# Order of the query tiles within an attention head: long and short tiles in turn instead of ascending

## The chip, the cores and the metric

One Trainium2 chip, one of its cores. The metric is the device time of one execution of the whole program, in microseconds (us); of several executions the median is given. Engines are named as the profile names them: PE is TensorE (PEld its weight loads), DVE VectorE, ACT ScalarE, POOL GpSimd, SP the queue that issues most DMAs. TensorE runs at one of two clock levels, 2.4 GHz and 1.2 GHz; the profile shows which was granted.

## The reference

Two decoder layers over 1024 tokens of width 1024, batch 1, in float32. Each layer projects the normed input once and splits the result among three token mixers: MLA attention (4 heads), GLA and RWKV-7; their outputs are joined, projected and added, and a gated convolutional FFN follows. The change is in the attention, which is causal, in query blocks of 128:

```python
for i in range(S // Q_BLOCK):
    end = (i + 1) * Q_BLOCK
    qb = q[:, i * Q_BLOCK:end]
    s = jnp.einsum('bqhd,bkhd->bhqk', qb, k[:, :end], preferred_element_type=jnp.float32)
    mask = (i * Q_BLOCK + local)[:, None] >= jnp.arange(end)[None, :]
    p = jax.nn.softmax(jnp.where(mask, s, -jnp.inf), axis=-1)
    outs.append(jnp.einsum('bhqk,bkhd->bqhd', p.astype(v.dtype), v[:, :end]))
```

Query block i meets i+1 key blocks, so block 7 is eight times the work of block 0. The blocks do not depend on each other.

## The kernel before

The program is one function, run once for each of the two layers: input projections, then a stage in which attention and the RWKV-7 recurrence run together, then the output projection (line 1424), then the FFN. The change touches the middle stage alone.

In that stage the outer loop goes over the 4 heads (h) and the inner one over the 8 query tiles (i). For a tile, `scores` writes q times k into a two-bank PSUM tile `psb` with matmuls of at most 512 columns (line 97; five for each run of columns, three of them `kn,qn` and two of them `khh,QP` and `kll,QP`). There are two such `psb` tiles. DVE adds the causal mask (L1119), takes the row maximum (L1121) and scales it (L1122); ACT takes the exponential into `p` (L1124). `trans` transposes `p` on PE, 128 columns at a time (L1135), and `pv` multiplies by v (L1146). The three run one tile apart: after the scores of a tile come the transposes of the tile before and the `pv` of the one before that (`flush`). A tile with i+1 key blocks asks for i+1 transposes and i+1 `pv` products. A `pv` product is a float32 matmul, which the trace records twice.

The weights of the next head are loaded and split by `dense_w` (L990, L992, L994) after the fourth tile of a head, and multiplied at its last tile (`dense_k`, `dense_q`).

The RWKV-7 recurrence is a generator, `rwkv_chunks`, over 8 pairs of chunks. It is resumed step by step: `spend` adds an estimate of PE time after each piece of attention, in proportion to i+1, and resumes the generator once for each 0.9 of it. Its steps are many small matmuls (L807, L821/L822, L832, L838, L852, L862, L879, L896, L900, L926) with a DVE or ACT step between them: L821 and L822 transpose in two groups of four, each into its own PSUM tile `psr`, DVE copies a group out (L825), and L832 follows; L807 is masked by DVE into `SC` (L811, two of them), which L879 reads. There are two `psr` tiles. When the heads are done, `drain` runs out what is left.

In head 3 a second generator, `early_wout`, prepares the output projection, which begins with tokens 0 to 127.

The order in which a loop records instructions is not the order in which an engine runs them: the framework schedules all engines by a simulated timeline and then fixes each engine's order. So PE's order in this stage is a mixture of attention, recurrence and projections, and a changed loop order moves all of it.

Of the kernel before, what the change touches and what calls it, by code (L numbers as in the profile page):

```python
# [21 lines left out]
NT = T // 128  # L22
# [39 lines left out]
def trunk(ctx: ExitStack, tc: tile.TileContext, A, out, offs):  # L62
# [241 lines left out]
    for l in range(DEPTH):  # L304
# [692 lines left out]
        def pg(tag, name, dt=F32, bufs=1):  # L997
            return ap.tile([128, T], dt, tag=tag, name=name, bufs=bufs)
# [83 lines left out]
        def dense_w(h):  # L1082
            return (w_small(2, 128, [(0, WKV[:, 256 * h:256 * h + 128])]),
                    w_small(3, 128, [(0, WQ[:, 192 * h:192 * h + 128])]))

        def dense_k(h, w):
            ps = bigps()
            mtile(ps, 128, 2, w, ckv)
            ps = halves(ps)
            kn = [pg(f"kn{j}", f"kn{j}", F32R) for j in range(2)]  # L1090
            for n in range(2):
                N = HALF[n]
                dve.tensor_tensor(ps[n], ps[n], Rk[:, N], ALU.mult)
                act.activation(kn[0][:, N], ps[n], AF.Copy)
                dve.tensor_tensor(kn[1][:, N], ps[n], kn[0][:, N].bitcast(F32), ALU.subtract)
            return kn

        def dense_q(h, w):
            ps = bigps()
            mtile(ps, 128, 3, w, cq)  # L1100
            ps = halves(ps)
            qn = [pg(f"qn{j}", f"qn{j}", F32R) for j in range(2)]
            for n in range(2):
                N = HALF[n]
                act.activation(qn[0][:, N], ps[n], AF.Copy)
                dve.tensor_tensor(qn[1][:, N], ps[n], qn[0][:, N].bitcast(F32), ALU.subtract)
            return qn

        def scores(h, i):
            kn, qn, qp = heads[h]  # L1110
            tk = slice(i * 128, (i + 1) * 128)
            nk = (i + 1) * 128
            s = bigps()
            for n0 in range(0, nk, 512):
                ks = slice(n0, min(max(nk, n0 + 256), n0 + 512))
                mm3(s[:, ks], (qn[0][:, tk], qn[1][:, tk]), (kn[0][:, ks], kn[1][:, ks]), True, False)
                mmr(s[:, ks], qp[:, tk], khh[:, ks], False, False)
                mmr(s[:, ks], qp[:, tk], kll[:, ks], False, True)
            dve.tensor_tensor(s[:, tk], s[:, tk], C("mdiag"), ALU.add)  # L1119
            sm = ap.tile([128, 4], F32, tag="sm", name="sm", bufs=4)  # L1120
            dve.tensor_reduce(sm[:, 0:1], s[:, 0:nk], AX.X, ALU.max, negate=True)  # L1121
            dve.tensor_scalar(sm[:, 1:2], sm[:, 0:1], rq[:, i:i + 1], None, ALU.mult)  # L1122
            p = pg("P", "p", bufs=2)
            act.activation(p[:, 0:nk], s[:, 0:nk], AF.Exp, scale=rq[:, i:i + 1], bias=sm[:, 1:2], accum_out=sm[:, 2:3])  # L1124
            dve.reciprocal(sm[:, 3:4], sm[:, 2:3])
            spend(0.27 * (i + 1))
            return p, sm
# [69 lines left out]
        def early_wout():  # L1197
            for k in range(3):
                wout_w(k)
                yield  # L1200
                yield
            prep_load(0)
            for k in range(3, 5):
                wout_w(k)
                yield
                yield
# [5 lines left out]
        def flush(n):  # L1212
            nonlocal t1, t2
            if n and t1 is not None:
                nt = (*t1[:2], trans(t1[1], t1[2]), t1[3])
            else:
                nt = None
            if t2 is not None:
                pv(*t2)
            t1, t2 = None, nt  # L1220

        for h in range(4):
            for i in range(NT):
                if h == 3 and i == 0:
                    bg.append(early_wout())
                r = scores(h, i)
                if h < 3 and i == 3:
                    wts = dense_w(h + 1)
                if i == NT - 1 and h < 3:
                    kn = dense_k(h + 1, wts[0])  # L1230
                    flush(1)
                    t1 = (h, i, *r)
                    qn = dense_q(h + 1, wts[1])
                    if h == 0:
                        heads[1] = (kn, qn, QP[1])
                        Q2 = [None, None]
                        Q2[0] = pg("QP0", "QPr", F32R)
                        nc.sync.dma_start(out=Q2[0].bitcast(F32), in_=qdr[0])
                    elif h == 1:
                        heads[2] = (kn, qn, Q2[0])  # L1240
                        Q2[1] = pg("QP1", "QPr", F32R)
                        nc.sync.dma_start(out=Q2[1].bitcast(F32), in_=qdr[1])
                    else:
                        heads[3] = (kn, qn, Q2[1])
                else:
                    flush(1)
                    t1 = (h, i, *r)
# [521 lines left out]
```

## Time and profile before

| what | us |
|---|---|
| median of 3 runs | 2701.03 |
| lowest and highest of them | 2699.57, 2706.45 |
| the profiled execution | 2708.75 |
| span of its profile | 2707.0 |
| PE busy in the span | 2620.6 (97%) |
| DVE busy | 1693.5 (63%) |
| ACT busy | 1145.0 (42%) |
| POOL busy | 1040.7 (38%) |

The profile is of one execution, and times in its rows are us from the start of its span. A busy PE is not a PE at its peak: matmuls are pipelined, their ends are modelled, and a matmul at 1.2 GHz is busy twice as long. The stage of the change runs from about 371 to 595 us in layer 0 and from about 1712 to 1940 us in layer 1.

### The profile page before, as it was taken

What the parts mean: (1) busy time and instruction counts of PE and PEld (TensorE: products, weight loads), DVE (VectorE), ACT (ScalarE), POOL (GpSimd) and SP (SyncE); (2) the same over time, 40 slices, a digit from 0 to 9 for tenths busy, and PEclk for the clock granted to TensorE, in tenths of its full rate; (3) what the DMA queues carried; (4) which work ended last, traced back from release to release, by engine and by line L of the source; (5) the groups of instructions that cost most, each with busy time, mean ns of one, the idle gap of its engine ahead of it and who ended that gap; (6) DMA issues with size and microseconds to landing.
All of it is one profiled execution on the core that took longest, in us unless ns stands there. A gap on an engine that the chain in (4) does not pass through costs nothing.

```text
span 2707.0 us, 35550 instructions
## 1 busy us (share of the span) xinstructions
PE 2620.6 (97%) x13586; PEld 2129.8 (79%) x13586; DVE 1693.5 (63%) x2404; ACT 1145.0 (42%) x1880; POOL 1040.7 (38%) x907
## 2 busy tenths in 40 slices
PE   8999999999999999999999999999999999999997
PEld 7668788888778888777776787888887788887786
DVE  3446565555976666777733665556469766668785
ACT  4221244454444544533352223444544454545433
POOL 3446432232554444221234553222325554542311
PEclk9999989999999999999999999799999999999999
DMA  4102121133232222684411122211332222216951
GB/s 130 32 24 68 56 70 41 33 126 125 78 100 73 94 72 70 210 202 119 122 30 32 32 71 70 54 34 42 129 130 66 94 84 80 94 55 220 211 129 63
DMA packets 246267, 240.90 MB, mean 89 GB/s; under 512 B 40312, under 2 KB 188240, under 8 KB 246096
## 3 DMA queue, kind: packets, MB, share of 16 engines
q1 hardware_dynamic: 210752, 203.31, 23.5%
q0 software_dynamic: 14336, 27.27, 5.8%
q10 hardware_dynamic: 21008, 8.04, 1.2%
q8 instruction: 107, 1.75, 0.3%
q14 instruction: 64, 0.52, 0.1%
HBM read 178.80 MB, written 53.48 MB: 86 GB/s over the span
## 4 chain that ended last, share of the span: by engine, by line
PE 76%; DVE 10%; DMA 4%; issue 4%; ACT 3%; POOL 3%; SPq 0%; POOLq 0%; DVEq 0%; ACTq 0%
PE psb L97 24%; PE psr L97 19%; PE psa L97 17%; PE psa L1146 2%; DMA R<-in_ffn_w_down 2%; PE psa L1135 1%; DMA R<-fdr 1%; PE psr L896 1%; PE psr L862 1%; PE psr L807 1%; DVE Tb L701 1%; DVE Ttmp L699 1%; DVE RG L1282 1%; PE psa L503 1%; PE psr L900 1%
## 5 line engine op out<-in xcount | busy, mean ns | idle before, releaser
L97 PE MATMUL psb<-hh,wh 128*128 128x512 f32 (+2 forms) x704 | 266.3, 380 | 5.3 <-ACT acc L748 3.9
L97 PE MATMUL psb<-hl,wh 128*128 128x512 f32 (+2 forms) x704 | 269.2, 383 | 1.6 <-DVE hl L208 1.6
L97 PE MATMUL psb<-hh,wl 128*128 128x512 f32 (+2 forms) x704 | 268.6, 382 | 1.8 <-POOL wl L258 1.8
L97 PE MATMUL psr<-B,RG 128*128 128x512 f32 x1032 | 253.9, 391 | 0.2
L97 PE MATMUL psa<-T,RG 128*128 128x512 f32 x1008 | 247.3, 391 | 1.0 <-ACT RG L1281 1.0
L97 PEld LDWEIGHTS psr<-B,RG 128*128 128x128 f32 x1032 | 193.4, 188 | 43.2 <-DVE RG L1282 1.0
L1282 POOL TENSOR_TENSOR RG<-S_m,RG 128x512 fp32r<-128x512 f32 x86 | 121.4, 1411 | 274.2 <-ACT RG L1281 239.5
L97 PEld LDWEIGHTS psa<-T,RG 128*128 128x128 f32 x1008 | 189.7, 188 | 42.8 <-ACT RG L1281 1.8
L1281 ACT ACTIVATE RG<-S_m 128x512 fp32r<-128x512 f32 x176 | 111.0, 630 | 227.0 <-PE psa L97 119.1
L97 PEld LDWEIGHTS psb<-hh,wh 128*128 128x128 f32 (+1 forms) x704 | 132.0, 188 | 35.0 <-issue 4.9
L97 PEld LDWEIGHTS psb<-hh,wl 128*128 128x128 f32 (+1 forms) x704 | 132.1, 188 | 34.4 <-issue 10.5
L97 PEld LDWEIGHTS psb<-hl,wh 128*128 128x128 f32 (+1 forms) x704 | 132.3, 188 | 29.6 <-issue 5.4
L97 PE MATMUL psr<-T,RG 128*128 128x512 f32 x528 | 137.4, 402 | 11.0 <-ACT T L1281 9.2
L97 PEld LDWEIGHTS psr<-T,RG 128*128 128x128 f32 x528 | 101.9, 194 | 35.7 <-ACT T L1281 10.1
L258 POOL TENSOR_TENSOR wl<-ws,wh 128x1024 fp32r<-128x1024 f32 (+1 forms) x40 | 91.2, 2281 | 95.8 <-ACT wh L256 61.3
L1479 DVE SCALAR_TENSOR_TENSOR psb<-uv,convc,psb 128x1023 f32<-128x1023 f32 x72 | 92.6, 1287 | 55.2 <-ACT psb L1477 54.2
L1281 ACT ACTIVATE de<-R 128x1024 fp32r<-128x1024 f32 x67 | 69.1, 1052 | 123.0 <-DMA R<-fdr 40.7
L1282 DVE TENSOR_TENSOR de<-R,de 128x1024 fp32r<-128x1024 f32 x67 | 86.2, 1303 | 43.9 <-ACT de L1281 43.9
L1589 POOL DMA_DIRECT2D R<-fdr x48 | 44.6, 982 | 176.8 <-issue 45.8
L97 PE MATMUL psb<-de 128*128 128x512 f32 x384 | 107.6, 399 | 5.0 <-DVE acc_kb L1660 5.0
L1479 DVE SCALAR_TENSOR_TENSOR psb<-ug,convc,psb 128x1023 f32<-128x1023 f32 x72 | 92.4, 1283 | 24.9 <-ACT psb L1477 23.9
L254 POOL TENSOR_TENSOR ws<-ws,pcol 128x1024 f32<-128x1024 f32 x36 | 74.3, 2068 | 82.3 <-DMA ws<-in_w_in 78.0
(549 smaller groups left out, 6626.0 us busy)
## 6 DMA issues: line engine op xcount, KB each, us to landing
wu_m<-in_ffn_w_up SPq DMA_DIRECT2D x88, 512.0 KB
fdr<-acc SPq DMA_DIRECT2D x44, 512.0 KB
R<-fdr SPq DMA_DIRECT2D x88, 256.0 KB
R<-in_ffn_w_down SPq DMA_DIRECT2D x88, 256.0 KB
ws<-in_w_in SPq DMA_DIRECT2D x38, 512.0 KB
R<-fdr POOLq DMA_DIRECT2D x48, 256.0 KB, 6.5
y_m<-ydr SPq DMA_DIRECT2D x16, 512.0 KB
xmid<-x SPq DMA_DIRECT2D x16, 512.0 KB
```

Of the source, the lines that this page charges most:

```text
L97: pe.matmul(o, lhsT=l, rhs=r, start=first, stop=last, skip_group_check=on)
L254: eng.tensor_tensor(ws, ws, g.rearrange("p (k o) -> p k o", o=1).to_broadcast([128, K, M]), ALU.mult)
L258: eng.tensor_tensor(wl, ws, wh.bitcast(F32), ALU.subtract)
L503: pe.matmul(pu[:, 0:256], lhsT=keT[r, i, :], rhs=vT[i // 4][r, i % 4, :], start=True, stop=True)
L699: dve.tensor_tensor(t3, Tb[:, 0:k, k:k + 1].to_broadcast([128, k, w]), Ub[:, k:k + 1, k + 1:32].to_broadcast([128, k, w]), ALU.mult)
L701: dve.tensor_tensor(Tb[:, 0:k, k + 1:32], Tb[:, 0:k, k + 1:32], t3, ALU.add)
L807: pe.matmul(pss[h2][:, o:o + 128], lhsT=kb[hf][p // 4][rows, 2 * (p % 4) + cc].rearrange("p a s -> p (a s)"), rhs=var[hf][p // 4][rows, 2 ...
L1146: pe.matmul(po[:, 0:128], lhsT=pT[:, j * 128:(j + 1) * 128], rhs=v[:, j, h * 128:(h + 1) * 128], start=(j == 0), stop=(j == i))
L1281: act.activation(d[0], s, AF.Copy)
L1282: eng.tensor_tensor(d[1], s, d[0].bitcast(F32), ALU.subtract)
L1479: dve.scalar_tensor_tensor(a[:, d:T], u[:, 0:T - d], conv[:, 2 - d, jj:jj + 1], a[:, d:T], ALU.mult, ALU.add)
L1589: pool.dma_start(out=o, in_=x, accum_op=ALU.add)
```

## The change

Within heads 0 to 2 the tiles go 7, 0, 6, 1, 5, 2, 4, 3, and within head 3 they go 0, 7, 1, 6, 2, 5, 3, 4. What was tied to the first, the fourth or the last tile of a head is tied to the first, fourth or last place in the new order. No arithmetic changes.

```diff
+
+        MIX = (7, 0, 6, 1, 5, 2, 4, 3)
         for h in range(4):
-            for i in range(NT):
-                if h == 3 and i == 0:
+            for n, i in enumerate(MIX if h < 3 else (0, 7, 1, 6, 2, 5, 3, 4)):
+                if h == 3 and n == 0:
                     bg.append(early_wout())
                 r = scores(h, i)
-                if h < 3 and i == 3:
+                if h < 3 and n == 3:
                     wts = dense_w(h + 1)
-                if i == NT - 1 and h < 3:
+                if n == NT - 1 and h < 3:
                     kn = dense_k(h + 1, wts[0])
                     flush(1)
                     t1 = (h, i, *r)
```

Every engine runs the same instructions as before, in another order within this stage. Three places matter below. The first is PE at the start of head 0 in layer 0 (`rcb` and `SC` are the recurrence's buffers, `kn`, `qn`, `khh`, `kll` and `QP` hold keys and queries). Before:

```order
L852 MATMUL psr<-rcb 32x32 x8
L97 MATMUL psb<-kn_2649,qn_2788 128x256
L97 MATMUL psb<-kn_2650,qn_2788 128x256
L838 MATMUL psr<-rcb,SC 64x64 x8
L97 MATMUL psb<-kn_2649,qn_2789 128x256
L896 MATMUL psr<-rcb,SC 128x64 x4
L900 MATMUL psr<-St_2340,rcb 128x128 x2
L862 MATMUL psr<-rcb 64x128 x4
L97 MATMUL psb<-kn_2649,qn_2788 128x256
L97 MATMUL psb<-kn_2650,qn_2788 128x256
L97 MATMUL psb<-kn_2649,qn_2789 128x256
L862 MATMUL psr<-rcb 64x128 x4
```

After:

```order
L852 MATMUL psr<-rcb 32x32 x8
L838 MATMUL psr<-rcb,SC 64x64 x8
L896 MATMUL psr<-rcb,SC 128x64 x4
L900 MATMUL psr<-St_2340,rcb 128x128 x2
L862 MATMUL psr<-rcb 64x128 x4
L97 MATMUL psb<-kn_2649,qn_2788 128x512
L97 MATMUL psb<-kn_2650,qn_2788 128x512
L97 MATMUL psb<-kn_2649,qn_2789 128x512
L97 MATMUL psb<-kn_2649,qn_2788 128x256
L97 MATMUL psb<-kn_2650,qn_2788 128x256
L97 MATMUL psb<-kn_2649,qn_2789 128x256
L862 MATMUL psr<-rcb 64x128 x4
```

The six 256-column score matmuls of tiles 0 and 1 have become three of 512 (first half of tile 7) and three of 256 (tile 0), in one run. The second place follows a little later on PE, from the first matmuls with `QP` on. Before:

```order
L97 MATMUL psb<-khh,QP_2495 128x256
L97 MATMUL psb<-kll,QP_2495 128x256
...
L807 MATMUL psr<-t_va_524,t_kb_520 128x128
L1135 MATMUL psa<-cst,p 128x128
L97 MATMUL psb<-kn_2649,qn_2788 128x384
L97 MATMUL psb<-kn_2650,qn_2788 128x384
L97 MATMUL psb<-kn_2649,qn_2789 128x384
L97 MATMUL psb<-khh,QP_2495 128x384
L97 MATMUL psb<-kll,QP_2495 128x384
L879 MATMUL psr<-SC,rcb 64x128 x6
```

After, ahead of and behind the same eight L807 matmuls:

```order
L97 MATMUL psb<-khh,QP_2495 128x512
L97 MATMUL psb<-kll,QP_2495 128x512
L97 MATMUL psb<-kn_2649,qn_2788 128x512
L97 MATMUL psb<-kn_2650,qn_2788 128x512
L97 MATMUL psb<-kn_2649,qn_2789 128x512
L97 MATMUL psb<-khh,QP_2495 128x512
L97 MATMUL psb<-kll,QP_2495 128x512
L97 MATMUL psb<-khh,QP_2495 128x256
L97 MATMUL psb<-kll,QP_2495 128x256
...
L879 MATMUL psr<-SC,rcb 64x128 x8
L926 MATMUL psr<-g2s,t_sg 128x256
L1135 MATMUL psa<-cst,p 128x128 x8
```

Ahead of L807 stand 4096 score columns where there were 1024 (four matmuls of 256); behind it nothing stands between L807 and L879. DVE's order there, after the change:

```order
L1121 TENSOR_REDUCE sm<-psb 128x1
L1119 TENSOR_TENSOR psb<-psb,cst 128x128
L929 TENSOR_TENSOR rcb<-rcb,st 128x256
L811 TENSOR_TENSOR SC<-psr,cst 128x4x128
L1122 TENSOR_SCALAR sm<-sm,rq 128x1
L1121 TENSOR_REDUCE sm<-psb 128x1
L811 TENSOR_TENSOR SC<-psr,cst 128x4x128
```

Two steps of the softmax, L1122 and L1121, stand between the two L811. The third place is PE at the last chunk pair of the recurrence. Before (the same in both layers):

```order
L1135 MATMUL psa<-cst,p 128x128 x3
L1146 MATMUL psa<-v,pT 128x128 x2
L821 MATMUL psr<-cst,t_va_523 128x128
L822 MATMUL psr<-cst,hat 128x128
L821 MATMUL psr<-cst,t_va_525 128x128
...
L822 MATMUL psr<-cst,hat 128x128
L832 MATMUL psr<-rcb,SC 32x32 x8
L838 MATMUL psr<-rcb,SC 64x64 x8
```

After, in layer 1:

```order
L821 MATMUL psr<-cst,t_va_10747 128x128
L822 MATMUL psr<-cst,hat 128x128
L821 MATMUL psr<-cst,t_va_10749 128x128
L822 MATMUL psr<-cst,hat 128x128
L1146 MATMUL psa<-v,pT 128x128
L97 MATMUL psb<-kn_14740,qn_14784 128x256
L97 MATMUL psb<-kn_14741,qn_14784 128x256
L97 MATMUL psb<-kn_14740,qn_14785 128x256
L97 MATMUL psb<-khh,QPr 128x256
L97 MATMUL psb<-kll,QPr 128x256
L832 MATMUL psr<-rcb,SC 32x32 x8
```

Before, the eight L821/L822 run straight into L832; after, a `pv` product and a tile's scores stand between (in layer 0 thirteen projection matmuls and a transpose do).

## Rows read from the trace of the kernel before

**Rows 1.** The page's first part: busy us, share of the span, instructions.

```profile
PE 2620.6 (97%) x13586; PEld 2129.8 (79%) x13586; DVE 1693.5 (63%) x2404; ACT 1145.0 (42%) x1880; POOL 1040.7 (38%) x907
```

**Rows 2.** Busy time by stretch: stretch, length, engines in the order named, granted clock, DMA.

```profile
core 0: us, PE busy (x) PEld busy (x) DVE busy (x) ACT busy (x) POOL busy (x), PEclk, DMA share, GB/s
372.71:389.77 17.06, 16.93 (x75) 14.78 (x73) 12.54 (x25) 6.00 (x13) 4.04 (x5) 0.50 0.05 12
1714.14:1738.04 23.90, 23.77 (x100) 19.79 (x101) 15.40 (x37) 7.84 (x18) 7.24 (x9) 0.50 0.05 12
1898.46:1901.88 3.42, 3.42 (x14) 3.13 (x13) 0.00 (x0) 3.32 (x8) 1.33 (x3) 0.50 0.05 19
389.80:595.00 205.20, 203.55 (x1619) 177.44 (x1618) 118.76 (x309) 101.34 (x227) 54.57 (x79) 1.00 0.19 60
1738.00:1895.00 157.00, 156.52 (x1263) 136.49 (x1262) 91.30 (x242) 74.37 (x172) 34.81 (x51) 1.00 0.13 38
```

**Rows 3.** Whom PE waited for, layer 0's stage: total us, times, longest.

```profile
PE psr L832 <- DVE SC L825: 0.8, 1, 0.8
PE psa L1135 <- ACT p L1124: 0.5, 1, 0.5
```

**Rows 4.** PE in order of time, layer 0's start: start us, us, work [idle before].

```profile
371.85 1.28 PE L838 MATMUL psr<-rcb,SC 64*64 64x64 f32 x16
...
379.02 1.96 PE L862 MATMUL psr<-rcb 64*64 64x128 f32 x8
381.12 1.97 PE L896 MATMUL psr<-rcb,SC 128*128 128x64 f32 x8
...
383.70 0.56 PE L97 MATMUL psb<-khh,QP 128*128 128x256 f32 x1
...
384.83 3.09 PE L807 MATMUL psr<-t_va,t_kb 64*128 64x128 f32 x16
...
387.99 1.31 PE L97 MATMUL psb<-kn,qn 128*128 128x384 f32 x3
...
389.85 0.63 PEld L879 LDWEIGHTS psr<-SC,rcb 64*64 64x64 f32 x12 [0.42 <-DVE rcb L929]
```

**Rows 5.** PE in order of time, the same place in layer 1.

```profile
1724.49 0.56 PE L97 MATMUL psb<-khh,QP 128*128 128x256 f32 x1
...
1736.95 1.36 PE L97 MATMUL psb<-kn,qn 128*128 128x512 f32 x3
```

**Rows 6.** Groups by shape on DVE and ACT, layer 0's stage: busy us, mean ns | idle.

```profile
L1119 DVE TENSOR_TENSOR psb<-psb,cst 128x128 f32<-128x128 f32 x32 | 9.4, 298 | 13.8 <-PE psb L97 13.3
L811 DVE TENSOR_TENSOR SC<-psr,cst 128x512 f32<-128x512 f32 x12 | 8.3, 689 | 2.8 <-PE psr L807 2.6
L1122 DVE TENSOR_SCALAR sm<-sm,rq 128x1 f32<-128x1 f32 x32 | 6.5, 210 | 0.5
L1121 DVE TENSOR_REDUCE sm<-psb 128x1 f32<-128x1024 f32 x4 | 4.9, 1225 | 0.8 <-ACT o L1149 0.7
L1121 DVE TENSOR_REDUCE sm<-psb 128x1 f32<-128x128 f32 x4 | 1.2, 291 | 0.1
L1124 ACT ACTIVATE p<-psb,sm,rq 128x1024 f32<-128x1024 f32 x4 | 4.8, 1203 | 0.4 <-DVE sm L1122 0.3
```

**Rows 7.** PE in order of time at full clock, layer 0, head 0 to 1.

```profile
442.15 1.08 PE L862 MATMUL psr<-rcb 64*64 64x128 f32 x8
443.16 1.10 PE L896 MATMUL psr<-rcb,SC 128*128 128x64 f32 x8
...
447.22 1.16 PE L807 MATMUL psr<-t_va,t_kb 64*128 64x128 f32 x8
```

**Rows 8.** PE in order of time, last chunk pair of layer 1.

```profile
1895.47 0.27 PE L822 MATMUL psr<-cst,hat 128*128 128x128 f32 x1
1896.57 0.69 PE L832 MATMUL psr<-rcb,SC 32*32 32x32 f32 x16 [0.83 <-DVE SC L825]
```

**Rows 9.** POOL in order of time: the weight split for a coming head.

```profile
428.57 1.00 POOL L994 TENSOR_TENSOR wl<-ws,wh 128x384 fp32r<-128x384 f32 x1 [0.27 <-ACT wh L992]
```

## The prediction

> **What bounds the kernel now.** I read the busy shares first [rows 1]: PE is busy for 97% of the span. A share over the whole span says little about one stage, so I read busy time by stretch next. From 389.80 to 595 us of layer 0 PE is busy 203.55 of 205.20 us at full clock, and from 1738 to 1895 us of layer 1 156.52 of 157.00 us; DVE and ACT lie below 60% in both [rows 2]. The waits of PE confirm it: in layer 0's whole stage the view names 0.8 us behind L825 and 0.5 us behind the exponential [rows 3]. The reader should see that the stage is bound by PE, that the recurrence and the projections fill what the softmax leaves open, and that an order of tiles cannot make PE's list shorter: every tile asks for the same matmuls in either order.
>
> What an order can change is the rate at which PE works off its list. Here the stretches tell something the waits do not: from 372.71 to 389.77 us and from 1714.14 to 1738.04 us the granted clock was 0.50, that is 1.2 GHz, though PE was busy 16.93 of 17.06 and 23.77 of 23.90 us; a third such stretch of 3.42 us lies at 1898.46 [rows 2]. PE at half clock does half the work, so these three cost 8.5, 12.0 and 1.7 us. In time order they begin while PE runs the recurrence's narrow matmuls (L838 on 64 rows and 64 columns, L862) with short score matmuls between them [rows 4], the third behind a wait of 0.83 us [rows 8]; the clock is back after the 384-column scores that begin at 387.99 us in layer 0 [rows 4] and during a run of 512-column scores in layer 1 [rows 5]. The change is worth what it makes of these three places.
>
> **The start of head 0.** Between L838 and the first `QP` matmul the order now holds the same recurrence and 3 x 512 + 3 x 256 = 2304 score columns instead of 6 x 256 = 1536. 768 columns more at 1.2 GHz are 0.64 us, so the `QP` matmuls, which began at 383.70 and 1724.49 us [rows 4, 5], now begin near 384.3 and 1725.1. There follow 7 x 512 + 2 x 256 = 4096 score columns without a break, 3.4 us at 1.2 GHz, to 387.7 and 1728.5. Such a run is what stood at the clock's return before; I take it that the clock is back at its end. Low clock would then end 2.1 us sooner in layer 0 and 9.5 us in layer 1, 11.6 us in all, of which half, **5.8 us, is won**. If the run does not bring the clock back, nothing is won: the bounds are -5.8 and 0.
>
> The columns drawn ahead are missed behind L807. Before, the five 384-column matmuls stood between L807 and L879 and covered DVE's masking; L879 waited 0.42 us [rows 4]. Now L879 follows L807 directly, and on DVE stand L811, L1122, L1121 of tile 0, L811: 0.689 + 0.210 + 0.291 + 0.689 = 1.88 us [rows 6]. Behind L879 are queued L926 and tile 7's eight transposes, so all of PE waits. 1.88 - 0.42 = 1.46 us in each layer, **2.9 us lost**. A wait of this size is what preceded the third low stretch [rows 8], and narrow L879 follows it, so the clock may fall again: a stretch of 3.42 us costs 1.7. I take **1.7 us** for one of the two layers, with bounds of 0 and 3.4.
>
> **The end of the recurrence.** The wait of L832 for L825 (0.8 us in layer 0, 0.83 in layer 1 [rows 3, 8]) comes from eight L821/L822 that run straight into L832. The new order has other matmuls between them at this place in both layers: 1.6 us won. The low clock at 1898.46 follows this wait; if it goes too, 1.7 more. **-3.3 us**, bounds -3.3 and 0. The wait can move to another chunk pair, but nowhere in the new order do the eight run undivided into L832.
>
> **Tile 7's softmax.** Where a long tile was followed by a long one, it is now followed by a short one, and its chain has less cover: mask 0.298, maximum 1.225, scaling 0.210, exponential 1.203, together 2.94 us [rows 6]. I counted in the new order what PE has between tile 7's last wide score matmul and its first transpose. In head 1 of layer 0, the tightest kind: five 256-column scores of tile 0, two L862 of 8 records, an L896, an L900 and four L807. The rows of these shapes give 2 x 1.08 + 1.10 + 1.16 = 4.4 us without scores and L900 [rows 7]. So 1.5 us of slack remain. If another DVE job is in the way, a wait like the 0.5 us of [rows 3] returns; I take one, **+0.5 us**, with bounds of 0 and 4 (one in each of eight heads).
>
> **Edits costed at nothing.** The weights of the next head are recorded after 18 of 36 key blocks instead of 10. Their split ends with 1.00 us on POOL [rows 9], and half a head, some 25 us of a 205 us stage with four heads [rows 2], still covers it; uncovered it would be about 1 us for each of six heads. The attention's output DMAs are as many as before. Their last tile is now tile 4, where it was tile 7, but tiles 0 and 1, which the output projection takes first, are still among the first three, and tile 4 waits behind four tiles of 48 matmuls each, 10 us a tile at 2.4 GHz. The background steps are resumed as often in a head, only earlier in it.
>
> **Sum.** -5.8 + 2.9 + 1.7 - 3.3 + 0.5 = -4.0 us. On the profiled execution's 2708.75 us that is 2704.8; that execution lies 7.7 us above the median shown, 2701.03, so against the median I expect **2697**. The bounds add up to -6.2 (-5.8 + 2.9 - 3.3) and +10.3 (2.9 + 3.4 + 4). 0.3% is 8.1 us, about what a measurement of this kernel can tell from no change.
>
> **Rivals.** *The clock returns at the first run already (19%).* The six matmuls of 2304 columns ahead of the second L862 could suffice. They would end about 4.7 us before the `QP` matmuls, since the second L862 and an L896 take 4.7 us from 379.02 to 383.70 [rows 4], near 379.6 and 1720.4. Then 10.2 + 17.6 us of low clock go, half of it won: -13.9 + 2.9 - 3.3 + 0.5 = -13.8, 2687. For it: a run of this length stands nowhere in the low stretch before. Against it: narrow L862 and L896 follow at once.
>
> *Long tiles are no longer covered (8%, slower).* If the real softmax chain is slower than the fixed order allows, each long tile stops PE between its scores and its transposes. Without the recurrence, a tile of 5 x 256 columns covers 0.5 us of 2.94. Half of the remaining 2.4 us on the four long tiles of eight heads is 32 x 1.2 = 38 us, less 4.0: 2735. It decides from 0.4 us a tile on (8.1 + 4.0 over 32). Against it: the fillers counted above, and the 0.5 us of [rows 3].
>
> *A new low stretch (4%, slower).* If the wait at L879 brings down the clock for as long as before, 17 us in each layer, 17 us are lost and only the end is won: 2701 + 17 + 2.9 - 3.3 = 2718.
>
> *PE's busy time hides waits (4%, faster).* The weight loads are busy 177.44 us where the matmuls are busy 203.55, and 136.49 where they are 156.52 [rows 2]. If this difference, 26.1 + 20.0 = 46 us, were waits inside matmuls, a smoother order could win part of it; a third is 15 us, 2686.
>
> The Trainium skill says so of the measure: its page "Trainium Kernel Development and Optimization", section "Performance Expectations", calls matmul busy time a bad metric of how near a kernel is to its limit, because matmuls are pipelined, and points to the busy share of the weight loads. By that rule the sum would start from 46 us of room in place of none. The trace bears it out only in part: loads are below matmuls in every stretch, but the view of waits names some 1.3 us.
>
> *The forecast: no change that can be told (65%)*, 2693 to 2709. That the order stays what it was is excluded; it does move on every engine.
>
> **How the numbers follow.** Faster by over 0.3%: 19 + 4 = 23%. Slower: 8 + 4 = 12%. The same: 65%. The range reaches down to 2686, into the first rival, and up to 2711, the upper bound of the sum; outside lie the slower rivals and little of the faster ones.
>
> **What the profile after would show.** Right: low clock in layer 1's start ends near 1729, not 1738; L879 idles near 1.9 us behind L811; no wait of L832 for L825 at the last chunk pair; PE busy over 99% between. Wrong: waits of L1135 for the exponential that add up to several us; a low stretch behind L879; low clock as long as before.

## The result and the profile after

The changed kernel takes 2725.89 us (median of four runs, 2722.38 to 2731.97), the kernel before 2702.26 on the same chip (2699.57 to 2706.45): a ratio of 1.0079, 95% interval 1.0062 to 1.0096. It is slower, by more than the 0.3% that can be told here. Measured a second time, on another occasion, the ratio is 1.0064 (1.0048 to 1.0080), 15.0 us between the medians (f1 below). I had forecast 2697 and no change that can be told.

The profiled execution after has a span of 2720.6 us, the one before 2707.0: 13.6 us to explain. The first part of the page after answers [rows 1]:

```profile
PE 2619.9 (96%) x13586; PEld 2128.9 (78%) x13586; DVE 1690.9 (62%) x2404; ACT 1142.5 (42%) x1880; POOL 1045.7 (38%) x907
```

PE is busy as long as before (2620.6). What was not busy is 2707.0 - 2620.6 = 86.4 us before and 2720.6 - 2619.9 = 100.7 after, 14.3 us more, and the mean granted clock is 0.979 in both. So the loss is idle time of PE; the next question is where.

To compare the two I cut both programs at the same amounts of PE work: I added up, in PE's order, the usual distance from one matmul to the next at full clock (0.227 us for one of 512 columns, and so on), and looked up when PE reached a given sum. For each layer's attention that gives three stretches: the start (sums 250 to 310, and 1480 to 1550 in layer 1), the middle (to 440, 1640) and the end (to 520, 1720), which reaches into the output projection. Busy time by stretch, the kernel before, first layer 0, then layer 1 (stretch, length, then busy us of the engines, granted clock, DMA):

```profile
322.90:400.20 77.30, 74.34 (x486) 61.46 (x484) 44.27 (x82) 36.03 (x73) 31.49 (x36) 0.87 0.29 77
400.20:543.00 142.80, 142.32 (x1150) 123.88 (x1147) 80.57 (x212) 65.05 (x150) 29.48 (x44) 1.00 0.12 36
543.00:627.60 84.60, 83.11 (x544) 71.39 (x544) 45.33 (x92) 43.59 (x85) 27.10 (x41) 1.00 0.39 131
...
1690.70:1781.70 91.00, 88.87 (x640) 75.67 (x639) 53.08 (x123) 42.02 (x93) 25.45 (x31) 0.85 0.19 52
1781.70:1881.10 99.40, 98.92 (x784) 85.19 (x783) 56.37 (x149) 45.73 (x105) 21.29 (x32) 1.00 0.12 33
1881.10:1967.70 86.60, 85.11 (x571) 74.02 (x570) 48.35 (x101) 44.14 (x89) 25.62 (x37) 0.98 0.36 119
```

The same pieces of work after the change:

```profile
323.40:399.50 76.10, 69.29 (x493) 57.17 (x492) 43.32 (x76) 33.78 (x65) 31.49 (x36) 0.93 0.29 76
399.50:541.70 142.20, 142.14 (x1163) 123.98 (x1162) 80.49 (x220) 64.20 (x152) 34.92 (x52) 1.00 0.11 31
541.70:633.30 91.60, 85.78 (x525) 72.84 (x523) 47.18 (x90) 46.75 (x91) 21.64 (x33) 0.98 0.39 130
...
1698.20:1786.20 88.00, 83.99 (x630) 71.63 (x629) 52.12 (x118) 39.02 (x86) 26.58 (x31) 0.90 0.19 53
1786.20:1889.20 103.00, 101.64 (x805) 88.81 (x803) 57.61 (x157) 44.00 (x107) 24.54 (x37) 0.97 0.09 24
1889.20:1980.70 91.50, 86.07 (x560) 73.04 (x559) 49.51 (x99) 46.47 (x93) 22.91 (x34) 0.98 0.37 122
```

The reader should see three things. The starts became shorter, by 1.2 and 3.0 us. The middle is as it was in layer 0 (142.8 and 142.2) and 3.6 us longer in layer 1. The ends became longer by 7.0 and 4.9 us, and there PE idles 5.82 and 5.43 us where it idled 1.49 each time. The rest of the program is 2.9 us longer. The sum is 13.6.

What PE waits for in layer 0's stage (total us, times, longest), to be read against [rows 3] (the view before also lists shorter waits of 0.5, 0.3 and 0.3 us in that stage, which [rows 3] leaves out):

```profile
PE psr L879 <- DVE SC L811: 2.5, 2, 2.3
PE psb L97 <- ACT p L1124: 2.4, 2, 1.5
...
PE psr L97 <- ACT RG L1176: 1.2, 1, 1.2
PE psa L1146 <- ACT pT L1137: 0.9, 1, 0.9
PE psr L97 <- DVE RG L1177: 0.5, 1, 0.5
```

L879 lies at the start of the stage. The other four are new and lie at its end. PE in order of time at the end of layer 0's stage, after the change:

```profile
567.34 0.97 PE L97 MATMUL psb<-kn,qn 128*128 128x512 f32 x3 [0.90 <-ACT p L1124]
...
572.15 0.71 PE L1146 MATMUL psa<-v,pT 128*128 128x128 f32 x4 [0.86 <-ACT pT L1137]
...
574.68 1.65 PE L97 MATMUL psb<-kn,qn 128*128 128x512 f32 x3 [1.49 <-ACT p L1124]
...
591.44 2.17 PE L1146 MATMUL psa<-v,pT 128*128 128x128 f32 x18
593.36 0.95 PE L97 MATMUL psr<-wo_kb,yhl_m 128*128 128x512 f32 x3
595.52 0.73 PE L97 MATMUL psr<-RG,yhl_m 128*128 128x512 f32 x2 [1.21 <-ACT RG L1176]
```

Scores wait until an exponential has read one of the two score buffers `psb`; then the output projection waits for its weights in `RG`, the blocks that can be written only once the attention's buffers are free. ACT there, first before the change, then after:

```profile
586.63 0.37 ACT L1149 ACTIVATE o<-psa,sm 128x128 f32<-128x128 f32 x1 [1.42 <-PE psa L1146]
...
587.40 2.01 ACT L1176 ACTIVATE RG<-wos 128x1024 fp32r<-128x1024 f32 x2 [0.40 <-DMA x<-in_x]
```

```profile
593.64 0.37 ACT L1149 ACTIVATE o<-psa,sm 128x128 f32<-128x128 f32 x1 [0.75 <-PE psa L1146]
...
594.41 2.01 ACT L1176 ACTIVATE RG<-wos 128x1024 fp32r<-128x1024 f32 x2 [0.40 <-ACT o L1149]
```

In both, `RG` is copied right behind the last output `o` of the attention. What differs is what PE has left to do meanwhile. PE before the change:

```profile
583.08 3.51 PE L1146 MATMUL psa<-v,pT 128*128 128x128 f32 x30
586.34 2.33 PE L97 MATMUL psr<-wo_m,yhl_m 128*128 128x512 f32 x9
588.51 1.04 PE L204 MATMUL psb<-cst,y_m 128*128 128x128 f32 x8
...
590.76 2.97 PE L97 MATMUL psr<-RG,yhl_m 128*128 128x512 f32 x12
```

Before, 15 L97 and 8 L204, 4.2 us, stood between the attention's last product and the first matmul on `RG`; after, three L97, 0.95 us. The others had been drawn ahead to fill the last tiles, because something else was no longer there. Counted in PE's fixed order of layer 0, 38 rows of attention and projection follow the recurrence's last L926 before the change, up to the attention's last L1146, and 130 follow it after. The recurrence's last L926 stands after 472 us of PE work before and after 460 after the change: it runs ahead, and the last tiles lose their filler.

Layer 1 is not the same. There the last L926 stands only some 3 us of work earlier after the change, and 77 rows follow it up to the last L1146 (38 before). No scores wait for an exponential; PE waits for the recurrence's own state and for the projection's weights:

```profile
PE psr L900 <- DVE St L904: 1.8, 1, 1.8
PE psr L97 <- ACT RG L1176: 1.7, 1, 1.7
...
PE psr L97 <- DVE RG L1177: 0.7, 1, 0.7
PE psr L97 <- DVE wo L1177: 0.6, 1, 0.6
```

### The profile page after: what moved, and what is told of

Read it like the earlier page. It is cut to its first block, busy times and chain, and to the rows that moved or that the text cites. A ratio compares the mean times of both kernels' runs of the same rounds, so it can differ in the third digit from the quotient of the medians.

```text
span 2720.6 us, 35564 instructions
## 1 busy us (share of the span) xinstructions
PE 2619.9 (96%) x13586; PEld 2128.9 (78%) x13586; DVE 1690.9 (62%) x2404; ACT 1142.5 (42%) x1880; POOL 1045.7 (38%) x907
## 3 DMA queue, kind: packets, MB, share of 16 engines
q1 hardware_dynamic: 210752, 203.31, 23.6%
## 4 chain that ended last, share of the span: by engine, by line
PE 43%; DVE 6%; DMA 3%; issue 2%; ACT 2%; POOL 1%; SPq 0%; ACTq 0%; POOLq 0%; DVEq 0%
PE psb L97 15%; PE psr L97 10%; PE psa L97 10%; PE psa L1146 1%; DMA R<-in_ffn_w_down 1%; DMA R<-fdr 1%; PE psr L862 1%; PE psa L1135 1%; PE psr L896 0%; DVE Ttmp L699 0%; PE psr L807 0%; DVE de L1284 0%; DVE Tb L701 0%; PE psr L838 0%; DVE RG L1284 0%
## 5 line engine op out<-in xcount | busy, mean ns | idle before, releaser
L97 PE MATMUL psb<-hh,wh 128*128 128x512 f32 (+2 forms) x704 | 266.3, 380 | 5.3 <-ACT acc L748 3.6
L97 PE MATMUL psb<-hl,wh 128*128 128x512 f32 (+2 forms) x704 | 269.8, 384 | 0.8 <-DVE hl L208 0.8
L97 PE MATMUL psb<-hh,wl 128*128 128x512 f32 (+2 forms) x704 | 268.8, 382 | 1.4 <-POOL wl L258 1.4
L97 PE MATMUL psr<-B,RG 128*128 128x512 f32 x1032 | 253.9, 391 | 0.4 <-DVE RG L1284 0.4
L97 PE MATMUL psa<-T,RG 128*128 128x512 f32 x1008 | 246.8, 390 | 1.0 <-ACT RG L1283 1.0
L97 PEld LDWEIGHTS psr<-B,RG 128*128 128x128 f32 x1032 | 193.4, 188 | 43.7 <-DVE RG L1284 1.2
L97 PEld LDWEIGHTS psa<-T,RG 128*128 128x128 f32 x1008 | 189.3, 188 | 42.7 <-ACT RG L1283 1.8
L97 PEld LDWEIGHTS psb<-hh,wh 128*128 128x128 f32 (+1 forms) x704 | 132.2, 188 | 35.1 <-issue 4.9
L97 PEld LDWEIGHTS psb<-hh,wl 128*128 128x128 f32 (+1 forms) x704 | 132.5, 188 | 34.1 <-issue 10.5
L97 PEld LDWEIGHTS psb<-hl,wh 128*128 128x128 f32 (+1 forms) x704 | 132.5, 188 | 28.9 <-issue 5.4
L97 PE MATMUL psr<-T,RG 128*128 128x512 f32 x528 | 137.4, 402 | 11.0 <-ACT T L1283 9.2
L97 PEld LDWEIGHTS psr<-T,RG 128*128 128x128 f32 x528 | 101.9, 193 | 35.7 <-ACT T L1283 10.1
L97 PE MATMUL psb<-de 128*128 128x512 f32 x384 | 107.5, 398 | 8.4 <-DVE acc_kb L1662 8.0
L254 POOL TENSOR_TENSOR ws<-ws,pcol 128x1024 f32<-128x1024 f32 x36 | 76.7, 2133 | 86.4 <-DMA ws<-in_w_in 77.5
L1481 DVE SCALAR_TENSOR_TENSOR psb<-ug,convc,psb 128x1023 f32<-128x1023 f32 x72 | 92.3, 1283 | 24.9 <-ACT psb L1479 23.9
L256 ACT ACTIVATE wh<-ws 128x1024 fp32r<-128x1024 f32 (+2 forms) x44 | 43.7, 994 | 151.6 <-PE psb L97 142.7
```

The lines of the kernel that those rows point to most:

```text
L97: pe.matmul(o, lhsT=l, rhs=r, start=first, stop=last, skip_group_check=on)
L254: eng.tensor_tensor(ws, ws, g.rearrange("p (k o) -> p k o", o=1).to_broadcast([128, K, M]), ALU.mult)
L256: act.activation(wh, ws, AF.Copy)
L1481: dve.scalar_tensor_tensor(a[:, d:T], u[:, 0:T - d], conv[:, 2 - d, jj:jj + 1], a[:, d:T], ALU.mult, ALU.add)
```

## The experiments

Theory 1 was that: the order in heads 0 to 2 lets the recurrence run ahead, and the end of the stage lacks cover. Theory 2 was head 3's own order, which makes a tile of middle length the last one; theory 3, that the alternation costs in every head. The table holds all of it: where the recurrence ends in layer 0's PE work, the ratio to the kernel before measured beside it, and from the profile the time lost in the start, middle and end of both stages (time to pass the stretch less the summed full-clock distances; a constant part is in it, so only differences count).

| kernel | ends at | ratio (95% interval) | start | middle | end | sum |
|---|---|---|---|---|---|---|
| before | 472 | 1 | 38.3 | 22.2 | 11.2 | 71.7 |
| f4 | 472 | 1.0008 (0.9996 to 1.0020) | 32.2 | 22.1 | 9.7 | 64.0 |
| changed | 460 | 1.0079 (1.0062 to 1.0096) | 34.1 | 25.2 | 23.1 | 82.4 |
| f1, changed again | 460 | 1.0064 (1.0048 to 1.0080) | 34.1 | 25.2 | 22.1 | 81.4 |
| e1 | 460 | 1.0032 (1.0018 to 1.0046) | 33.0 | 20.8 | 25.5 | 79.3 |
| e2 | 474 | 1.0031 (1.0017 to 1.0044) | 38.1 | 20.6 | 17.8 | 76.5 |
| e3 | 474 | 1.0000 (0.9987 to 1.0013) | 34.0 | 21.3 | 16.1 | 71.4 |
| e4 | 474 | 0.9992 (0.9979 to 1.0005) | 33.3 | 20.2 | 12.6 | 66.1 |
| f2 | 473 | 0.9998 (0.9984 to 1.0012) | 35.8 | 19.8 | 11.5 | 67.1 |
| f3 | 476 | 1.0051 (1.0037 to 1.0065) | 38.6 | 20.8 | 18.5 | 77.9 |
| h1 | 473 | 1.0006 (0.9990 to 1.0023) | 33.3 | 22.2 | 13.0 | 68.5 |
| h2 | 464 | 1.0009 (0.9993 to 1.0025) | 27.3 | 23.6 | 17.1 | 68.0 |
| i1 | 473 | 1.0017 (1.0002 to 1.0031) | 30.8 | 23.6 | 15.6 | 70.0 |
| i2 | 472 | 0.9989 (0.9977 to 1.0000) | 31.4 | 21.1 | 11.0 | 63.5 |

The five kernels whose time is slower by 0.3% or more have the five largest sums. How much a row varies by itself is seen where two profiles have the same order: before and f4 (the same order of PE up to the projection) differ by 6.1 us in the start and 1.5 in the end, the changed kernel and f1 by 1.0 in the end. So the end can be read more finely than the start and the sum.

**e1, heads 0 to 2 new, head 3 ascending.**

```diff
-for n, i in enumerate(MIX if h < 3 else (0, 7, 1, 6, 2, 5, 3, 4)):
+for n, i in enumerate(MIX if h < 3 else range(NT)):
```

> Heads 0 to 2 keep the new order, head 3 goes back to ascending. On PE the recurrence's last L926 stands after 460 us of matmul work in layer 0, as in the changed kernel (460), not as before the change (472). Theory 1 (with long and short tiles in turn the recurrence runs ahead, ends about 12 us of work too soon, and the last tiles of the stage have nothing beside them): most of the loss stays, 2715 to 2728 us, and PE's waits lie in the last 45 us of the stage. Theory 2 (head 3's own order, which makes tile 4 the last one, delays the output projection's weights and inputs): the loss goes, 2697 to 2708. Theory 3 (alternation costs everywhere in heads 0 to 2): 2715 to 2728 too, but the lost time lies spread over heads 0 to 2.

2715.80 us, ratio 1.0032. The loss of the middle isn't there (20.8); all of it lies in the end (25.5), and here the recurrence ends some 12 us of work early in both layers. So theory 3 falls, and theory 1 holds, though the time is half the loss and not most of it.

**e2, only head 3 new.** The side edit, the later load of y, keeps that load behind the outputs it reads.

```diff
-            prep_load(0)
             for k in range(3, 5):
                 wout_w(k)
                 yield
                 yield
+                if k == 3:
+                    prep_load(0)
...
-for n, i in enumerate(MIX if h < 3 else (0, 7, 1, 6, 2, 5, 3, 4)):
+for n, i in enumerate(range(NT) if h < 3 else (0, 7, 1, 6, 2, 5, 3, 4)):
```

> Heads 0 to 2 ascending, only head 3 in the new order 0, 7, 1, 6, 2, 5, 3, 4; the first load of y is recorded one weight block later. The recurrence's last L926 stands after 474 us of matmul work (472 before, 460 in the changed kernel). Theory 1 (recurrence ends too soon): like before, 2697 to 2708. Theory 2 (head 3's own order): slow, 2712 to 2728. Theory 3 (alternation in heads 0 to 2 costs everywhere): like before, 2697 to 2708.

2715.93 us, ratio 1.0031: head 3's own order costs too, so theory 2 is right beside theory 1. In layer 0 of its profile PE waits 1.58 us for an exponential (a score buffer) and 0.7 + 0.7 us for `RG`; in layer 1 there is neither, but a wait of 2.6 us for the last weights `wo`. On ACT, in order of time, one sees why `RG` comes late in layer 0:

```profile
587.88 0.37 ACT L1149 ACTIVATE o<-psa,sm 128x128 f32<-128x128 f32 x1 [2.81 <-PE psa L1146]
...
590.85 1.03 ACT L207 ACTIVATE yhl_sg<-psb 128x1024 fp32r<-128x1024 f32 x1 [2.60 <-PE psb L204]
591.77 2.00 ACT L1176 ACTIVATE RG<-wos 128x1024 fp32r<-128x1024 f32 x2
```

Before the change the copy into `RG` starts 0.4 us behind the last `o`. Here that `o` ends at 588.25, but L207, which waits for PE's L204, now stands ahead of it on ACT, and it starts 3.5 us behind.

**e3, new order, recurrence late.**

```diff
-Q_IN, Q_ATT, Q_OUT, ELIM = 2.4, 0.9, 1.6, 5
+Q_IN, Q_ATT, Q_OUT, ELIM = 2.4, 2.1, 1.6, 5
```

> The new order everywhere, but the recurrence and the other background steps are resumed every 2.1 of the estimate instead of every 0.9, so that they are recorded later and have a later rank. The recurrence's last L926 stands after 474 us of matmul work instead of 460. Theory 1 (recurrence ends too soon): the loss at the end of both stages (8.8 + 4.2 us in the profiles) goes, 2700 to 2713. Theory 2 (head 3's own order) and theory 3 (alternation costs everywhere): no change, 2718 to 2730.

2709.04 us where the kernel before takes 2707.80: the loss is gone. In the profile the end falls from 23.1 to 16.1 and not to 11: head 3's order is still there, and with it e2's waits for `RG` (0.7 + 0.7 us). In the time, though, nothing of e2's 0.31% is left, so head 3's order has no fixed price that stays whatever the rest does. The middle gives 3.9 as well.

**e4, tile 7 first in head 0, all else ascending.**

```diff
-for n, i in enumerate(MIX if h < 3 else (0, 7, 1, 6, 2, 5, 3, 4)):
+for n, i in enumerate((7, 0, 1, 2, 3, 4, 5, 6) if h == 0 else range(NT)):
```

> Ascending everywhere, except that tile 7 comes first in head 0: the part of the change that moves score columns to where the clock was low. The recurrence's last L926 stands after 474 us. If the low clock at the start of the stage is what the order can win, and the rest of the change is what loses: 0 to 4 us faster than before, 2697 to 2703, and the low stretches near 373 to 390 and 1714 to 1738 us are shorter. If moving tile 7 there brings a wait of its own that costs more (tile 7's softmax with only tile 0 behind it): 2704 to 2712.

2704.80 us, ratio 0.9992: no difference that can be told. The low stretches in the start are shorter, as the first reading expected (3.4 us from 387.6 us, 10.2 from 1718.8), but L879's wait is there in full (2.3 us).

**f1, the changed kernel again.** No edit.

> The changed kernel once more, beside the next three. If head 3's own order and heads 0 to 2 each cost what they cost alone (0.31 and 0.32% in e2 and e1), and the costs add up: 0.6% slower than before, some 17 us. If both lose the same cover at the end of the stage, so that the second finds little left to lose: 0.3 to 0.45%. If the first measurement holds: 0.79%, 0.6 to 1.0.

2722.00 us against 2707.01, ratio 1.0064: the sum of e1 and e2 (0.32 and 0.31%). That the costs add up is not shown by this, since in e3 head 3's order cost nothing that can be told.

**f2, e1 with the recurrence late.** e1's edit and e3's.

> Heads 0 to 2 in the new order, head 3 ascending as in e1, and the background steps resumed every 2.1 as in e3. The recurrence's last L926 stands after 473 us of matmul work instead of 460. Theory 1 (what e1 lost, it lost because the recurrence ends too soon): e1's 0.32% goes, ratio 0.996 to 1.001. If e1's loss is the alternation itself, wherever the recurrence stands: 1.002 to 1.005.

2706.95 us, ratio 0.9998: e1's loss is gone. The pair e1 and f2 has the same order of tiles and differs in the pacing of the background alone. PE's waits at the end of layer 0's stage, e1 first:

```profile
PE psb L97 <- ACT p L1124: 2.6, 1, 2.6
PE psr L97 <- ACT RG L1176: 1.9, 1, 1.9
PE psa L1135 <- ACT p L1124: 0.6, 1, 0.6
PE psr L97 <- DVE RG L1177: 0.5, 1, 0.5
...
```

```profile
PE psr L97 <- DVE wo L1177: 0.8, 1, 0.8
PE psa L1135 <- ACT o L1149: 0.5, 1, 0.5
PE psr L97 <- DVE x L1435: 0.4, 1, 0.4
```

The waits for the score buffer and for `RG` (L1176), 4.5 us, are gone. The pacing moves both background streams, the recurrence and in head 3 the preparation of the projection: behind the last L1146 there are now 30 L97 and 8 L204 before the first matmul on `RG`, where e1 has none. So the pair shows that the pacing of the background makes the loss, and not how much of it is the recurrence's.

**f3, ascending with the recurrence late.** e3's edit in the kernel before.

> The kernel before, ascending in every head, with the background steps resumed every 2.1: what e3's edit does by itself. The recurrence's last L926 stands after 476 us of work, 472 before. Theory 1: there is no early end to mend, ratio 0.998 to 1.003. If a late rank of the background steps is a gain in any order, e3's recovery says nothing of the recurrence's end: ratio 0.990 to 0.996.

2718.85 us, ratio 1.0051: slower, which neither reading expected. A late rank is no gain by itself, so e3's recovery is not that; but late can be too late. The recurrence's last steps now stand behind the attention's last L1146, and the projection starts late:

```profile
583.29 2.34 PE L97 MATMUL psr<-wo_m,yhl_m 128*128 128x512 f32 x9 [1.21 <-ACT rcb L905]
...
596.24 1.20 PE L97 MATMUL psr<-wo,yhl_m 128*128 128x512 f32 x4 [1.68 <-DVE wo L1177]
```

**f4, e2's side edit alone.** The later load of y, in the kernel before.

> The kernel before with e2's side edit alone: the first load of y recorded one weight block later. If e2's 0.31% is head 3's order: ratio 0.999 to 1.001. If it is the late load: 1.002 to 1.004.

Ratio 1.0008 (0.9996 to 1.0020): e2's loss is not the side edit's. Its profile is a second one of the ascending order, and shows how far the start varies by itself: 32.2 us lost, where the first one lost 38.3.

**h1, head 3 alternating with tile 7 last.** e2 with another order.

```diff
-(0, 7, 1, 6, 2, 5, 3, 4)
+(0, 4, 1, 5, 2, 6, 3, 7)
```

> Heads 0 to 2 ascending, head 3 in the order 0, 4, 1, 5, 2, 6, 3, 7: long and short in turn as in e2, but with tile 7 last. The first load of y is late as in e2. The recurrence's last L926 stands after 473 us of work; on ACT the two copies into RG (L1176) stand ahead of the second L207, as before the change, where e2 has L207 ahead of them. If e2's 0.31% came from how the end falls out (scores waiting for an exponential, RG's copies behind L207): ratio 0.998 to 1.0015. If turning long and short costs in head 3 by itself: 1.002 to 1.004.

Ratio 1.0006: e2's loss is gone with the alternation still there. It is how the end falls out that costs. The score wait is there once in each layer (1.1 and 1.4 us), the waits for `RG` are not.

**h2, heads 0 to 2 descending, head 3 ascending.**

```diff
-MIX = (7, 0, 6, 1, 5, 2, 4, 3)
+MIX = (7, 6, 5, 4, 3, 2, 1, 0)
...
-for n, i in enumerate(MIX if h < 3 else (0, 7, 1, 6, 2, 5, 3, 4)):
+for n, i in enumerate(MIX if h < 3 else range(NT)):
```

> Heads 0 to 2 in descending order, 7 to 0, so that nothing alternates; head 3 ascending. The recurrence's last L926 stands after 464 us of work (472 before, 460 in e1), and between the stage's last L1146 and the first matmul on RG stands nothing, as in e1, where before stood 15 L97 and 8 L204. Theory 1 (the early end of the recurrence costs): slower by 0.2 to 0.35%. If the alternation costs: ratio 0.998 to 1.0015. If long tiles with no cover between them cost: PE's waits for exponentials lie in heads 0 to 2, and more than 0.4% is lost.

Ratio 1.0009: a miss for theory 1 as I had put it in numbers. The profile keeps its mechanism and corrects its size. The recurrence ends at 464 and the wait for `RG` is there,

```profile
587.76 0.74 PE L97 MATMUL psr<-RG,yhl_m 128*128 128x512 f32 x2 [1.92 <-ACT RG L1176]
```

but no wait of scores in layer 0 and 0.9 us of it in layer 1, where e1 waits 2.6 us in layer 0: the end loses 17.1, some 6.6 more than the two ascending profiles (11.2 and 9.7), while e1 lost 15 more. The start, 27.3, is the best of all; that this pays for the end is not shown, since the start varies by 6 us in one order.

**i1, h2 with the recurrence late.** h2's edit and e3's.

> Heads 0 to 2 in descending order, head 3 ascending, and the background steps resumed every 2.1: the start of h2 (whose low clock ended at 378.8 and 1713.7 us) with the end of f2. The recurrence's last L926 stands after 473 us of work, 464 in h2, and behind the stage's last L1146 stand 30 L97 and 8 L204 before the first matmul on RG, where h2 has none. Theory 1: h2's waits for RG (2.4 us in each stage) go, and the kernel is faster than before by 0.1 to 0.4%, ratio 0.996 to 0.999. If the end is not what h2 lost: ratio as h2's, 0.9993 to 1.0025.

Ratio 1.0017: a miss. The waits for `RG` went, as expected, yet the end lost 15.6 still. At each end stands one wait of transposes for the exponential (1.2 and 1.1 us in the two layers), which f2 does not have there, and 3.4 us of low clock behind it, from 546.3 and 1894.5 us. (The expectation's 1713.7 us for the end of h2's low clock in layer 1 is a slip: it ended at 1723.7.)

**i2, only head 0 descending.**

```diff
-for n, i in enumerate(MIX if h < 3 else (0, 7, 1, 6, 2, 5, 3, 4)):
+for n, i in enumerate((7, 6, 5, 4, 3, 2, 1, 0) if h < 1 else range(NT)):
```

> Head 0 descending, heads 1 to 3 ascending. The recurrence's last L926 stands after 472 us of work and the end of the stage reads row for row as before the change. If a run of wide score matmuls at the start of head 0 shortens the low clock there, as in h2's profile: 0.05 to 0.3% faster than before, ratio 0.997 to 0.9995, with the low stretch that begins near 372 us shorter than 10 us. If the low clock there varies as it does between runs of the ascending order (13.7 to 17.1 us in layer 0, 13.7 to 23.9 in layer 1): ratio 0.999 to 1.001.

2704.30 us against 2707.48, ratio 0.9989 (0.9977 to 1.0000). The end is that of the ascending order (11.0). The low stretch from 373.7 us is 6.8 us long, but in layer 1 there are 13.7. It is the fastest of these kernels, by an amount that can't be told from none.

## Why the prediction was wrong

**The step that failed** stands under "Edits costed at nothing": "The background steps are resumed as often in a head, only earlier in it." That is so in the order in which the steps are recorded, and it is not what sets when PE runs them. The scheduled order lets each chunk pair follow the last after 22 to 28 us of PE work in layer 0 after the change (L926 at 302, 330, 356, 382, 407, 431, 453, 460), where it took 20 to 31 before (302, 333, 359, 388, 415, 446, 466, 472; the short last step apart). The recurrence gains 12 us in layer 0, some 3 in layer 1, and is missing where the last tiles need it. I had asked what the order does to each tile's cover and to head 0's start, and not what it does to the filler that was to last until the stage's end. The end, where I had priced a gain of 3.3 us and no cost, took 7.0 + 4.9 us of the profile's 13.6. f2 against e1 shows for heads 0 to 2 that the place of the background steps is the cause: with the same order of tiles, later steps take the ratio from 1.0032 to 0.9998. It is not the whole of it: i1, with steps as late, gained nothing on h2.

**The second half of the same part** failed with it: "Their last tile is now tile 4 [...] and tile 4 waits behind four tiles of 48 matmuls each". That is true of tile 4's output. But the projection also waits for the copy into `RG`, behind the last output `o` whatever its tile is, and its cover shrank from 4.2 to 0.95 us. h1 against e2 shows that head 3's loss does not come from turning long and short as such (ratios 1.0006 and 1.0031). That the late `RG` makes it is argued from the rows, not shown by itself.

**The start: the right sign, its size not to be told.** I had -5.8 + 2.9 + 1.7 = -1.2 for both layers together; the profiles say -1.2 and -3.0, that is -4.2. Term by term: low clock, after the change,

```profile
362.80:369.60 6.80, 6.21 (x17) 4.90 (x18) 4.36 (x11) 2.68 (x6) 0.00 (x0) 0.50 0.36 83
390.10:393.50 3.40, 3.40 (x14) 3.02 (x14) 1.79 (x8) 1.22 (x4) 2.07 (x3) 0.50 0.08 28
...
1721.30:1735.00 13.70, 13.53 (x68) 11.54 (x65) 7.63 (x13) 4.05 (x6) 5.08 (x5) 0.50 0.03 10
1844.20:1851.00 6.80, 6.80 (x27) 5.76 (x27) 1.93 (x6) 2.04 (x7) 0.00 (x0) 0.50 0.01 2
```

lasts 13.70 us in layer 1's start where it was 23.90 [rows 2]: 10.2 less, where I had 9.5. (Its end at 1735.0 cannot be set beside my 1728.5, since layer 1's start comes 7.5 us later after the change.) The run of score columns ended there at about 1734.4, so the clock came back just behind it, as I had taken. In layer 0 the stretch at 362.8 is not the one I had priced: PE's order is still the same there, and the profile before has one of 3.4 us at 362.5. The stretch priced did not come at all; from 369.6 to 390.1 us, ahead of the score columns and through them, the clock was at 2.4 GHz. In e1, whose PE order is that of the changed kernel up to 549 us, it did come, from 372.5 to 386.1 us, and ended within the run, which went from 383.3 to 386.6. So the mechanism fits two of these three places, and the rival by which the first run of columns suffices fits none (in e1 that run went from 376.6 to 378.9 us). But f4 has 13.7 us of low clock in both layers with the order of before, so the gain cannot be credited to the run. L879 waits 2.27 us for L811 in layer 0 (1.05 in e1), where I had 1.88, but only 0.2 in layer 1, where I had the same. (The 0.42 us that I took off lie before a weight load, not before a matmul, and L929 ended them, not L811 [rows 4].)

```profile
384.54 1.71 PE L807 MATMUL psr<-t_va,t_kb 64*128 64x128 f32 x16
388.52 1.09 PE L879 MATMUL psr<-SC,rcb 64*64 64x128 f32 x16 [2.27 <-DVE SC L811]
```

The new low stretch behind it came, 3.40 us at 390.1, in one of two layers as taken. None of this could be told from the times: three profiles whose starts have the ascending order lose 38.3, 32.2 and 33.3 us there (before, f4, h1), the changed kernel 34.1.

**The recurrence's end: right for the wait, luck for the clock.** The wait of L832 for L825 is gone in both layers, as forecast. The low stretch at 1898.46 is gone too, but f4, which has the wait of 0.8 us in both layers, doesn't have the stretch either, so its 1.7 us were no sure gain. Other waits and low stretches (574.4, 1926.1 us) took their place at the new end.

**Tile 7's softmax: right in the middle.** No L1135 waits for an exponential in the middle of the stage; PE is busy 142.14 of 142.20 us there in layer 0. Only at the end of layer 0 does a softmax lack cover: scores wait 2.4 us for an exponential and L1146 0.9 us for a copied transpose. So the slower rival, long tiles no longer covered in every head, is not what happened: the sign was its, the place was not. The rival of a new low stretch came only to the size in my sum.

**PE's busy time** was the rival from the Trainium skill's page "Trainium Kernel Development and Optimization", section "Performance Expectations", which calls it a bad metric. Here the weight loads, one of the two measures which that section prefers, say the same as the matmuls: 2129.8 us before and 2128.9 after, against 2620.6 and 2619.9. Both are unchanged, and the loss stood in the idle time where the view of waits names it; no gain came out of the loads' lower share.

**What stays open.** Layer 1's middle is 3.6 us longer: a wait of 0.68 us ahead of an L896 precedes the low stretch of 6.80 us above, half of which is lost; which edit brings it there wasn't tried. Why the scheduled recurrence moves faster when heads don't ascend was not tried either; h2 shows that it needs no alternation. The recurrence and the preparation of the projection were never paced apart. In layer 1 the recurrence ends only some 3 us early, so the 4.9 us lost there are explained less well than layer 0's 7.0. And two results do not fit a simple sum of costs: e3 keeps head 3's order and loses nothing that can be told, and i1 loses at its end although its recurrence ends late. Last, the profiles explain 13.6 us where the two measurements say 15 to 24; the rest I can't place.

## What to carry to other kernels

Where a background stream fills the gaps of a bound stage, look at what an order does to the stream's last step: ask first how much filler is left for the last tiles, in the scheduled order and not in the code's. The step's place alone does not give the time: in e2 and i1 it stood at 474 and 473, as in kernels that lost nothing, and their ends lost 17.8 and 15.6 us against 11.2 before. An edit in the middle of a stage can be neutral there and be paid at its end, at the hand-over to the next stage, where buffers come free. And too late can be as bad as too soon: the same edit of the pacing won 0.3% in one order (f2 against e1), lost 0.5% in another (f3), and changed nothing that can be told in a third (i1 against h2).

## What the runs showed of the hardware

The same order of PE's instructions at the start of the stage met low clock, at 1.2 instead of 2.4 GHz, for 17.1 and 23.9 us in one profile (before, from 372.7 and 1714.1 us), for 13.7 and 13.7 in another (f4, from 373.7 and 1715.1) and for 10.2 and 13.7 in a third (h1, from 378.2 and 1723.0). Between the first two that is 6.8 us of time. The changed order varied too: e1, with the same order of PE up to 549 us, had 13.7 us of low clock from 372.5 us, the changed kernel none until 390.1. A forecast from one profile's low stretches carries that much uncertainty. In layer 0 after the change the clock stayed at 2.4 GHz through two idle spells of 1.29 and 0.51 us near 380 us, and fell at 390.1 us, 1.6 us after the 2.27 us wait of L879 had ended.
